# The end of a depthwise convolution on one core: who sums the last chunks' taps, and what the layer norm's queue holds

## The chip, the core and the metric

The kernel runs on one core of a Trainium2 chip. The metric is the device time of one execution in microseconds (us); the number for a kernel is the median of its runs. TensorE is called PE in the profile, VectorE DVE, ScalarE ACT, GpSimd POOL, and SyncE's queue, which issues the weight loads, SPq.

## The reference

A two-layer trunk over 256 tokens of width 2048, in float32. Layer 0 mixes with a convolution module, layer 1 with latent attention, and each is followed by a squared-ReLU MLP of width 8192. Only the convolution module of layer 0 matters here:

```python
def conv_module(h, w_pw1, b_pw1, w_dw, b_dw, ln_g, ln_b, w_pw2, b_pw2):
    u = h @ w_pw1 + b_pw1                     # 2048 -> 4096
    a, gate = jnp.split(u, 2, axis=-1)
    u = a * jax.nn.sigmoid(gate)
    u = causal_depthwise_conv(u, w_dw) + b_dw # 31 taps, every channel by itself
    u = jax.nn.silu(layer_norm(u, ln_g, ln_b))
    return u @ w_pw2 + b_pw2                  # 2048 -> 2048
```

The layer norm takes mean and variance over all 2048 channels of a token, so nothing of it, and nothing of the second product (pw2), can start before the last channel of the depthwise sum is there.

## The kernel before

**Numbers.** Products are done in split float32: each operand is cut into a high part (`hi`, a rounded copy made on ScalarE) and a low part (`lo` = value minus `hi`, made on VectorE or GpSimd), and three matmuls hi·hi, lo·hi and hi·lo are summed. `split_half` (L152) does this for one half of a loaded weight group: `hi` at L158, `lo` at L159. A loaded group lies in one of three `raw` buffers, and the next load into that buffer waits until both halves have been cut.

**Tiling.** Channels are cut into 16 chunks (`KC`) of 128, tokens into two tiles of 128. Until the layer norm, data lie with channels on partitions and the 256 tokens along the free axis (`S` = 256).

**The conv stage** (L703 to L733) loops over chunks `c`, with the order of the instructions on every engine written out by hand (`manual_schedule`). In turn `c`, PE computes the pw1 product of chunk `c` (`conv_mm`, L483), while the other engines work on the chunk before: `glu(c-1)` (L501) makes the gated value `ub` from two accumulators (the sigmoid on ACT; the product on GpSimd, but on VectorE for the last chunk, L509), and the 31 taps of the depthwise sum follow. Of an ordinary chunk:

- ScalarE does tap 0 with the bias (L542) and a few more taps as separate products (`product`, L519), which GpSimd adds up (`side_sum`, L562);
- VectorE does the other taps, one multiply-add of 128x256 each (`dve_tap`, L586), and adds the GpSimd sum once (L569). `dve_taps` (L590) takes turns between the two oldest chunks that have taps left, so that one multiply-add needn't wait for the one just before it. It stops when `REST` or `LAST_REST` taps are left over all chunks; what is left is done in the next turn.

The last chunk (number 15) is different. `LAST_PE` = 22 of its taps are matmuls with diagonal weights (`diag`, L524, made on ScalarE; `last_products`, L534), 11 ahead of the transposes of chunk 13 and 11 behind; four are ScalarE products added by GpSimd; five are on VectorE, which adds all three parts at L583.

**Queues at the end.** Turn 16 has no pw1 product. VectorE's queue holds `glu(15)`, then the rest of chunks 13, 14 and 15. PE's queue holds the matmul taps, the transposes of chunk 13 (`to_tokens`, L617; its statistics `bn_stats`, L633, follow on VectorE), the rest of the matmul taps, then some dummy transposes (`keep_warm`, L220, with the counts `N_WARM_LN`) and the transposes of chunks 14 and 15.

**The layer norm** (L738 to L791). `bn_aggr` (L743) gives mean and variance of each token; `rsqrt` (L201) the scale, by a square root on ScalarE and one Newton step on VectorE; `spread` (L748) puts mean and scale across partitions with PE transposes; `ln_op` subtracts the mean or multiplies by the scale (L763); `ln_swish` does the SiLU on ScalarE (L771), its high part `sh` (L774), and its low part `sl` on VectorE (L775). `rsqrt` is used by every RMS norm but the final one as well; one of those calls stands ahead of the first product of the kernel.

**The pw2 product** (L792) then runs over the 16 values of `k`, two to a weight group. `NU` = 32 is the number of the first pw2 weight group; the groups 32 and 33 are loaded and partly cut before the layer norm. In the kernel before, the second half of group 33 is cut inside the loop, behind `ln_swish(4)` in ScalarE's queue.

Of the kernel before, what the change touches and what calls it, by code (L numbers as in the profile page):

```python
# [43 lines left out]
LAST_PE = 22  # L44
SIDE = 2
LAST_SIDE = (3, 6, 4)
# [3 lines left out]
LAST_REST = (20, 17, 0)  # L50
FILL_AT = (5, 15)
N_WARM = 14
N_WARM_LN = (8, 17, 6, 10)
# [23 lines left out]
def trunk_kernel(  # L77
# [74 lines left out]
    def split_half(raw, h, eng):  # L152
# [5 lines left out]
        nc.scalar.activation(hi, raw[:, js, :], AF.Copy)  # L158
        eng.tensor_tensor(lo, raw[:, js, :], hi.bitcast(F32), op=ALU.subtract)  # L159
        return hi, lo  # L160

# [39 lines left out]
    def rsqrt(ms, n, eps, name):  # L201
# [8 lines left out]
        nc.vector.tensor_tensor(t, t, v, op=ALU.mult)  # L210
        nc.vector.tensor_scalar(t, t, scalar1=-0.5, scalar2=1.5, op0=ALU.mult, op1=ALU.add)
        nc.vector.tensor_tensor(y, y, t, op=ALU.mult)
# [224 lines left out]
    with ExitStack() as cx:  # L437
# [32 lines left out]
        def conv_half(n, h):  # L470
            if n < NU + KC // 2:
                wjs[n, h] = split_half(raws[n], h, nc.gpsimd if 0 < n + h and (n, h) < (NU + 1, 1) else nc.vector)
# [44 lines left out]
        def product(c, w):  # L517
            pr = cv2.tile([P, S], F32, tag="tp", name=nm("tp"), bufs=sum(LAST_SIDE))
            nc.scalar.activation(pr, ubs[c][:, w : w + S], AF.Copy, scale=tap(c, w))  # L519
            return pr  # L520
# [10 lines left out]

        def last_products(w0, w1):
            for w in range(w0, w1):
                nc.tensor.matmul(  # L534
                    last_sum[0], dgs[w], ubs[KC - 1][:, w : w + S], start=w == 0, stop=w == LAST_PE - 1
                )

        def start_sum(c):
            w = 0
            if c < KC - 1:  # L540
                pcs[c] = sum_tile()[:, :S]
                nc.scalar.activation(  # L542
                    pcs[c], ubs[c][:, 0:S], AF.Identity, bias=b_dw[:, c : c + 1], scale=tap(c, 0)
                )
                w = 1
            else:
                pcs[c] = acc_tile()[:, :S]
                o = sum_tile()[:, :S]
                last_sum.append(o)
                last_products(0, LAST_PE // 2)  # L550
                w = LAST_PE
            n = n_side(c)
            sides[c] = [product(c, w + i) for i in range(n)]
            left[c] = list(range(w + n, W))
            left[c].insert(min(JOIN, len(left[c]) - 1), None)
# [8 lines left out]

        def dve_tap(c):
            w = left[c].pop(0)
            out = pcs[c]
            if w is None:
                nc.vector.tensor_tensor(out, out, sides[c][0], op=ALU.add)  # L569
                return  # L570
            if c == KC - 1 and w == LAST_PE + n_side(c):
                nc.vector.tensor_scalar(
                    out, ubs[c][:, w : w + S], scalar1=tap(c, w), scalar2=b_dw[:, c : c + 1],
                    op0=ALU.mult, op1=ALU.add,
                )
                return
            if not left[c]:
                if c == KC - 1:
                    half = cv2.tile([P, S], F32, tag="half", name=nm("half"), bufs=1)
                    nc.vector.scalar_tensor_tensor(  # L580
                        out=half, in0=ubs[c][:, w : w + S], scalar=tap(c, w), in1=out, op0=ALU.mult, op1=ALU.add
                    )
                    nc.vector.tensor_tensor(ca[:, c, :], last_sum[0], half, op=ALU.add)  # L583
                    return
                out = ca[:, c, :]
            nc.vector.scalar_tensor_tensor(  # L586
                out=out, in0=ubs[c][:, w : w + S], scalar=tap(c, w), in1=pcs[c], op0=ALU.mult, op1=ALU.add
            )

        def dve_taps(c, fill):  # L590
# [3 lines left out]
            lead = 0 if c in (0, KC - 1) else LEAD  # L594
            while sum(len(v) for v in left.values()) > rest(c):
# [3 lines left out]
                if ready[-1] == KC - 1 and len(left[KC - 1]) == 1 and len(ready) > 1:  # L599

                    ready.pop()
                k = next((k for k in ready[:2] if k != last), None)
                if fill and (k is None or n >= FILL_AT[c == KC - 1]):
# [4 lines left out]
                if c == KC - 1 and k == KC - 3 and not left[k]:  # L608

                    to_tokens(k)  # L610
                    last_products(LAST_PE // 2, LAST_PE)
                last = turns["last"] = k
                n += 1
            while fill:
                fill.pop(0)()

# [30 lines left out]
        with tc.manual_schedule():  # L647
# [55 lines left out]
            for c in range(1, KC + 1):  # L703
# [4 lines left out]
                if c < KC:  # L708
                    pss[c] = [acc_tile() for _ in range(2)]
                conv_half(n + (c < KC), 0)  # L710
                start_sum(c - 1)
                if c < KC:
                    conv_half(n + 1, 1)
                    dve_taps(c - 1, fill)
                    conv_load(n + 4)
                    side_sum(c - 1)
                    conv_mm(c, 0, 8)
                    if c < KC - 1:
                        conv_half(n + 2, 0)
                        conv_half(n + 2, 1)  # L720
                else:
                    side_sum(c - 1)
                    conv_half(n, 1)
                    conv_half(n + 1, 0)
                    dve_taps(c - 1, fill)
                    conv_load(n + 4)
                if c < KC:
                    conv_mm(c, 8)
                    if c > KC - 4:
                        dgs.extend(diag(KC - 1, w) for w in range(len(dgs), min(len(dgs) + 8, LAST_PE)))  # L730
                    if c > 2:
                        to_tokens(c - 3)
                    conv_mm(c, 12)  # L733
# [19 lines left out]
            rl = rsqrt(mv[:, :, 1], T, LN_EPS, "n")  # L753
# [6 lines left out]
            def ln_op(k, n, row, op):  # L760
                o = ca[:, k : k + n, :]
                row = row.rearrange("p (a n) -> p a n", a=1).broadcast_to([P, n, S])
                nc.vector.tensor_tensor(o, o, row, op=op)  # L763

# [18 lines left out]
            for row, op in ((mean, ALU.subtract), (scale, ALU.mult)):  # L783
                for k in range(2):
                    ln_op(k, 1, row, op)
            for k in range(2):
                ln_swish(k, 1)
            ln_norm(2)
            ln_swish(2)
            ln_norm(4)  # L790
            keep_warm(ident, N_WARM_LN[3])  # L791
            for m in range(NP):  # L792
# [4 lines left out]
                for j in range(2):  # L797
                    k = 2 * m + j
                    wh, wl = conv_w(NU + m, j)
                    for b in range(2):  # L800
                        bs = slice(b * NB, (b + 1) * NB)
                        for t in range(T):
                            mm3(ps2[b][t], sh_kt(k, t), sl_kt(k, t), wh[:, bs], wl[:, bs], k == 0, k == KC - 1)
                    if m == 0 and j == 0:
                        conv_half(NU + 1, 1)
# [600 lines left out]
```

## Time and profile before

| | us |
|---|---|
| median of three runs (lowest, highest) | 1997.01 (1995.37, 1997.14) |
| the profiled execution: its own time | 1997.01 |
| the profiled execution: span from the first to the last instruction | 1995.1 |
| PE busy, share of the span | 1970.5, 99% |
| DVE busy | 1219.0, 61% |
| ACT busy | 972.5, 49% |
| POOL busy | 223.9, 11% |
| mean granted TensorE clock | 0.998 |

Times in the views count from the start of the span. A row of the timeline gives start, duration, engine, line, operation, output and inputs, shapes, the count of instructions merged into the row, and in brackets how long the engine had been idle and what ended that. A float32 matmul of the depthwise taps (L534) stands in the trace as two records, so 22 records are 11 taps. The conv stage ends near 204 us, its depthwise sum near 218, and the pw2 product starts near 223.5.

### The profile page before, as it was taken

The numbers are of one execution on the slowest core, as the hardware profiler recorded it, in microseconds if no ns is written. First come the engines' busy times: TensorE is split into PE (matmuls) and PEld (weight loads), VectorE is DVE, ScalarE is ACT, GpSimd is POOL, SyncE is SP. The second block draws the span as 40 slices with busy tenths as digits, with TensorE's granted clock in tenths as the row PEclk, the third lists the DMA queues.
The fourth block names the chain that finished last, engine by engine and source line by source line (L and its number), as shares of the span: only waits on it lengthen the run. The fifth ranks groups of instructions, "written<-read, shape, count | busy, mean of one in ns | idle before, by whom it ended". The sixth has DMA issues, their size and how long they took to land.

```text
span 1995.1 us, 27788 instructions
## 1 busy us (share of the span) xinstructions
PE 1970.5 (99%) x11025; PEld 1726.1 (87%) x11025; DVE 1219.0 (61%) x1808; ACT 972.5 (49%) x1378; POOL 223.9 (11%) x184
## 2 busy tenths in 40 slices
PE   7999999999999999999999999999999999999998
PEld 7999788888888888888899998888888888888886
DVE  6999877556444555655556665656654545665553
ACT  5456655445333444544456665545443334454443
POOL 5999200000000000000001310000000000000000
PEclk9999999999999999999999999999999999999999
DMA  7666365665655666655555445666655666655553
GB/s 239 186 182 183 127 208 179 189 190 189 198 198 191 190 190 190 190 190 190 190 159 174 122 148 183 198 190 190 191 190 191 197 194 189 190 190 196 194 190 105
DMA packets 243265, 367.57 MB, mean 184 GB/s; under 512 B 15416, under 2 KB 89792, under 8 KB 242880
## 3 DMA queue, kind: packets, MB, share of 16 engines
q1 hardware_dynamic: 242400, 364.68, 58.0%
q8 instruction: 86, 1.41, 0.3%
q10 hardware_dynamic: 736, 1.12, 0.2%
q14 instruction: 43, 0.35, 0.0%
HBM read 363.68 MB, written 2.10 MB: 183 GB/s over the span
## 4 chain that ended last, share of the span: by engine, by line
PE 89%; DVE 8%; ACT 1%; DMA 0%; issue 0%; POOL 0%; SPq 0%; ACTq 0%; DVEq 0%
PE acc L403 23%; PE acc L184 16%; PE acc L186 16%; PE acc L185 16%; PE acc L404 12%; DVE sum L586 6%; PE acc L490 1%; PE acc L489 1%; PE acc L491 1%; PE tr L241 1%; PE sum L534 1%; DMA xs<-in_x 0%; ACT hi L158 0%; DVE lo L159 0%; PE acc L1180 0%
## 5 line engine op out<-in xcount | busy, mean ns | idle before, releaser
L159 DVE TENSOR_TENSOR lo<-raw,hi 128x1024 fp32r<-128x1024 f32 (+2 forms) x630 | 760.9, 1211 | 691.3 <-ACT hi L158 679.5
L158 ACT ACTIVATE hi<-raw 128x1024 fp32r<-128x1024 f32 (+1 forms) x696 | 723.3, 1046 | 790.0 <-PE acc L185 454.8
L403 PE MATMUL acc<-xt,hi 128*128 128x512 f32 x2048 | 710.6, 390 | 0.0
L404 PE MATMUL acc<-xt,lo 128*128 128x256 f32 x2048 | 577.7, 282 | 0.0
L403 PEld LDWEIGHTS acc<-xt,hi 128*128 128x128 f32 x2048 | 384.5, 188 | 80.5
L184 PE MATMUL acc<-hi,gh 128*128 128x512 f32 x1024 | 398.6, 389 | 0.0
L186 PE MATMUL acc<-lo,gh 128*128 128x512 f32 x1024 | 398.4, 389 | 0.0
L185 PE MATMUL acc<-hi,gl 128*128 128x512 f32 x1024 | 398.4, 389 | 0.0
L404 PEld LDWEIGHTS acc<-xt,lo 128*128 128x128 f32 x2048 | 387.1, 189 | 0.1
L186 PEld LDWEIGHTS acc<-lo,gh 128*128 128x128 f32 x1024 | 192.2, 188 | 40.1
L184 PEld LDWEIGHTS acc<-hi,gh 128*128 128x128 f32 x1024 | 192.2, 188 | 40.0
L185 PEld LDWEIGHTS acc<-hi,gl 128*128 128x128 f32 x1024 | 192.2, 188 | 39.2
L586 DVE SCALAR_TENSOR_TENSOR sum<-ub,w_dw,sum 128x256 f32<-128x256 f32 x400 | 162.7, 478 | 7.5 <-ACT sum L542 6.4
L159 POOL TENSOR_TENSOR lo<-raw,hi 128x1024 fp32r<-128x1024 f32 x66 | 157.6, 2408 | 22.0 <-ACT hi L158 22.0
L489 PE MATMUL acc<-xt,hi 128*128 128x256 f32 x512 | 144.4, 282 | 0.0
L491 PE MATMUL acc<-xt,lo 128*128 128x256 f32 x512 | 143.0, 279 | 0.3 <-POOL lo L159 0.3
L490 PE MATMUL acc<-xt,hi 128*128 128x256 f32 x512 | 143.0, 279 | 0.2 <-DVE xt L197 0.2
L491 PEld LDWEIGHTS acc<-xt,lo 128*128 128x128 f32 x512 | 96.2, 188 | 0.5 <-POOL lo L159 0.5
L490 PEld LDWEIGHTS acc<-xt,hi 128*128 128x128 f32 x512 | 96.3, 188 | 0.4 <-DVE xt L197 0.4
L489 PEld LDWEIGHTS acc<-xt,hi 128*128 128x128 f32 x512 | 96.3, 188 | 0.0
L975 POOL MEMSET pad_kv<- 128x8 f32 x1 | 0.1, 105 | 769.2 <-PE acc L186 769.2
L411 ACT ACTIVATE v<-acc 128x256 f32<-128x256 f32 x128 | 46.3, 381 | 25.4 <-PE acc L404 25.4
(240 smaller groups left out, 1780.4 us busy)
## 6 DMA issues: line engine op xcount, KB each, us to landing
raw<-in_mlp_w SPq DMA_DIRECT2D x256, 1024.0 KB, 5.2
raw<-in_conv_w_pw SPq DMA_DIRECT2D x64, 512.0 KB, 5.3
raw<-in_conv_w_pw SPq DMA_DIRECT2D x16, 1024.0 KB, 5.1
raw<-in_mla_w_o SPq DMA_DIRECT2D x16, 1024.0 KB, 5.7
raw<-in_mla_w_kv_up SPq DMA_DIRECT2D x8, 1024.0 KB, 5.6
raw<-in_mla_w_in SPq DMA_DIRECT2D x8, 576.0 KB, 3.7
raw<-in_mla_w_in SPq DMA_DIRECT2D x4, 1024.0 KB, 5.5
raw<-in_mla_w_q_up SPq DMA_DIRECT2D x16, 256.0 KB, 3.5
```

Source lines behind the costliest of these rows:

```text
L158: nc.scalar.activation(hi, raw[:, js, :], AF.Copy)
L159: eng.tensor_tensor(lo, raw[:, js, :], hi.bitcast(F32), op=ALU.subtract)
L184: nc.tensor.matmul(ps, sh, mh, start=start, stop=False)
L185: nc.tensor.matmul(ps, sl, mh, start=False, stop=False)
L186: nc.tensor.matmul(ps, sh, ml, start=False, stop=stop)
L403: nc.tensor.matmul(ps[b], wh[:, bs], xhl(k), start=k == 0, stop=False)
L404: nc.tensor.matmul(ps[b][:, :S], wl[:, bs], xh(k), start=False, stop=k == KC - 1)
L411: nc.scalar.activation(v[:, b, :], o[:, S:], AF.Copy)
L489: nc.tensor.matmul(o, wh[:, bs], xh(k), start=k == 0, stop=False)
L490: nc.tensor.matmul(o, wh[:, bs], xl(k), start=False, stop=False)
L491: nc.tensor.matmul(o, wl[:, bs], xh(k), start=False, stop=k == KC - 1)
L586: nc.vector.scalar_tensor_tensor(out=out, in0=ubs[c][:, w : w + S], scalar=tap(c, w), in1=pcs[c], op0=ALU.mult, op1=ALU.add)
```

## The change

- **Last chunk's taps.** `LAST_PE` falls from 22 to 20: 20 taps on PE, in two halves of 10. The other 11 (20 to 30) are all ScalarE products, the first with the bias, and GpSimd adds them up with ten additions. VectorE only adds the PE part and the GpSimd part.
- **Gap.** Before its first matmul tap PE gets 12 dummy transposes (`N_WARM_GAP`).
- **Chunks 13 and 14.** `dve_taps(14)` leaves 20 items instead of 17, so `glu(15)` stands three multiply-adds earlier on VectorE. A new function `dve_end` does the rest: the last four taps of chunk 13 in turns with three of chunk 14, then the last twelve of chunk 14 as two separate sums in turns (one of them starting from chunk 14's GpSimd sum, so that L569 falls away), which one addition joins. The statistics of chunk 13 come after 14 multiply-adds.
- **Weight groups 32 and 33.** The first half of 32 is cut in turn 15 (ScalarE behind the halves of group 31, GpSimd ahead of chunk 14's `side_sum`); its second half in turn 16 behind chunk 15's products and additions. The high parts of both halves of 33 (`upper_half`) are made in turn 16 on ScalarE, their low parts (`lower_half`) on VectorE behind `ln_swish(2)`; before, the low part of the first half was on GpSimd.
- **Layer norm.** `rsqrt` has one VectorE instruction less; the first subtraction of the mean stands inside it, between the square root and the reciprocal; `ln_norm(4)` moves ahead of `ln_swish(2)`; the counts of dummy transposes change from (8, 17, 6, 10) to (6, 13, 7, 13).
- **Order of the terms.** In pw2, for `k` = 0 the matmuls with the low part of the activations (`sl`) come behind the others of that `k`, for `k` = 2 those with the low part of the weights.

```diff
-LAST_PE = 22
+LAST_PE = 20
-LAST_SIDE = (3, 6, 4)
+LAST_SIDE = (3, 6, W - LAST_PE)
-LAST_REST = (20, 17, 0)
-FILL_AT = (5, 15)
+LAST_REST = (20, 20)
+FILL_AT = (5, 14)
-N_WARM_LN = (8, 17, 6, 10)
+N_WARM_GAP = 12
+N_WARM_LN = (6, 13, 7, 13)
...
-    def rsqrt(ms, n, eps, name):
+    def rsqrt(ms, n, eps, name, meanwhile=None):
...
         nc.scalar.activation(t, v, AF.Sqrt)
+        if meanwhile is not None:
+            meanwhile()
         nc.vector.reciprocal(y, t)
-        nc.vector.tensor_tensor(t, y, y, op=ALU.mult)
+        nc.vector.scalar_tensor_tensor(out=t, in0=y, scalar=-0.5, in1=y, op0=ALU.mult, op1=ALU.mult)
         nc.vector.tensor_tensor(t, t, v, op=ALU.mult)
-        nc.vector.tensor_scalar(t, t, scalar1=-0.5, scalar2=1.5, op0=ALU.mult, op1=ALU.add)
-        nc.vector.tensor_tensor(y, y, t, op=ALU.mult)
+        nc.vector.scalar_tensor_tensor(out=y, in0=t, scalar=1.5, in1=y, op0=ALU.add, op1=ALU.mult)
...
+        def start_last():
+            c = KC - 1
+            last_sum.append(sum_tile()[:, :S])
+            keep_warm(ident, N_WARM_GAP)
+            last_products(0, LAST_PE // 2)
+            sides[c] = [product(c, w, None if w > LAST_PE else b_dw[:, c : c + 1]) for w in range(LAST_PE, W)]
...
+        def dve_end(fill):
+            c, d = KC - 3, KC - 2
+            n = 0
+            left[d].remove(None)
+            while left[c]:
+                dve_tap(c)
+                if left[c]:
+                    dve_tap(d)
+                    n += 1
+                n += 1
+
+            to_tokens(c)
+            last_products(LAST_PE // 2, LAST_PE)
+            m = len(left[d]) // 2
+            first, second = left[d][:m], left[d][m:]
+            left[d] = []
+            out = acc_tile()[:, :S]
+            half = cv2.tile([P, S], F32, tag="half", name=nm("half"), bufs=1)
+            for i, w in enumerate(second):
+                add_tap(half if i == len(second) - 1 else out, d, w, sides[d][0] if i == 0 else out)
+                if i < len(first):
+                    add_tap(pcs[d], d, first[i], pcs[d])
+                n += 2
+                while fill and n >= FILL_AT[1]:
+                    fill.pop(0)()
+            nc.vector.tensor_tensor(ca[:, d, :], pcs[d], half, op=ALU.add)
+            nc.vector.tensor_tensor(ca[:, d + 1, :], last_sum[0], sides[d + 1][0], op=ALU.add)
...
+                if c == KC:
+                    start_last()
+                    side_sum(KC - 1)
+                    conv_half(NU, 1)
+                    uppers = [upper_half(raws[NU + 1], h) for h in range(2)]
+                    dve_end(fill)
+                    conv_load(n + 4)
+                    break
...
+                if c == KC - 1:
+                    conv_half(NU, 0)
...
-            for row, op in ((mean, ALU.subtract), (scale, ALU.mult)):
-                for k in range(2):
-                    ln_op(k, 1, row, op)
+            ln_op(0, 1, scale, ALU.mult)
+            ln_norm(1, 1)
             for k in range(2):
                 ln_swish(k, 1)
             ln_norm(2)
+            ln_norm(4)
             ln_swish(2)
-            ln_norm(4)
+            for h in range(2):
+                wjs[NU + 1, h] = lower_half(*uppers[h], nc.vector)
             keep_warm(ident, N_WARM_LN[3])
...
+                    late = {0: 1, 2: 2}.get(k)
+                    groups = [terms] if late is None else [terms[:late] + terms[late + 1 :], [terms[late]]]
...
-                    if m == 0 and j == 0:
-                        conv_half(NU + 1, 1)
```

More of the change, by code (lines that the diff above doesn't have):

```diff
@@ L150, in load, with upper_half @@
         return raw
-    def split_half(raw, h, eng):
+    def upper_half(raw, h):
         _, nj, cols = raw.shape
@@ L563, in side_sum, with add_tap @@
                 step *= 2
+        def add_tap(out, c, w, base):
+            nc.vector.scalar_tensor_tensor(
+                out=out, in0=ubs[c][:, w : w + S], scalar=tap(c, w), in1=base, op0=ALU.mult, op1=ALU.add
+            )
         def dve_tap(c):
             w = left[c].pop(0)
-            out = pcs[c]
             if w is None:
[L569 to L588, printed above, removed]
+                nc.vector.tensor_tensor(pcs[c], pcs[c], sides[c][0], op=ALU.add)
+            else:
+                add_tap(pcs[c] if left[c] else ca[:, c, :], c, w, pcs[c])
         def dve_taps(c, fill):
             n, last = 0, turns.get("last")
-            lead = 0 if c in (0, KC - 1) else LEAD
+            lead = 0 if c == 0 else LEAD
             while sum(len(v) for v in left.values()) > rest(c):
```

111 lines of the change are left out of this document (50 added, 61 removed).

## Prediction, made before the changed kernel was run

> **What bounds the kernel now.** I began with the engines' shares on the page and with PE's waits from the start of pw2 to the end.
>
> ```profile
> PE 1970.5 (99%) x11025; PEld 1726.1 (87%) x11025; DVE 1219.0 (61%) x1808; ACT 972.5 (49%) x1378; POOL 223.9 (11%) x184
> ...
> PE tr L1171 <- DVE pr L1165: 1.2, 2, 1.0
> PE acc L184 <- ACT hi L158: 0.6, 1, 0.6
> PE acc L184 <- ACT sh L774: 0.6, 1, 0.6
> PE acc L186 <- DVE lo L159: 0.5, 1, 0.5
> ```
>
> PE is busy 99% of the span, and from 223 us on it waits five times, for 2.9 us together; the three waits of L184 and L186 (1.7 us) lie at the start of pw2, as rows below show. So whatever brings pw2 forward brings the end forward, and the place to look is between the last pw1 matmul and the steady part of pw2. There the share misleads: PE counts as busy, but at half clock or with dummy transposes. The chain that ended last, cut to that stretch, tells the order:
>
> ```profile
> 197.00 8.24 DVE sum L586 x21
> 205.24 0.41 DVE ub L509
> ...
> 205.69 6.70 PE sum L534 x22
> 212.39 0.22 PE tr L624 x2
> 212.61 4.75 PE sum L534 x22
> 217.36 0.87 PE acc L224 x8
> 218.24 0.45 PE acc L624 x4
> ...
> 218.71 0.76 DVE stats L633 x2
> ```
>
> VectorE works through chunks 13 and 14 until it can start `glu(15)`; then 22 matmul taps on PE hold everything until 217.36. The first 11 take 6.70 us, the same count behind them 4.75. The windows (PE, PEld, DVE, ACT, POOL busy, then the granted clock) say why:
>
> ```profile
> 206.00:207.00 1.00, 1.00 (x4) 0.86 (x3) 1.00 (x4) 1.00 (x4) 1.00 (x1) 0.61 0.06 16
> 208.00:209.00 1.00, 1.00 (x4) 0.82 (x3) 1.00 (x4) 1.00 (x2) 1.00 (x2) 0.50 0.00 0
> 210.00:211.00 1.00, 1.00 (x7) 0.86 (x6) 1.00 (x4) 0.77 (x2) 1.00 (x1) 1.00 0.00 0
> ```
>
> The clock is 0.61, 0.50 and then 1.00. What precedes is in the timeline:
>
> ```profile
> 203.38 0.28 PE L491 MATMUL acc<-xt,lo 128*128 128x256 f32 x1
> 203.76 0.47 ACT L506 ACTIVATE sg<-acc,vecs 128x256 f32<-128x256 f32 x1 [3.71 <-PE acc L491]
> 205.19 0.45 DVE L509 SCALAR_TENSOR_TENSOR ub<-acc,vecs,sg 128x256 f32<-128x256 f32 x1
> 194.84 2.50 ACT L519 ACTIVATE tp<-ub,w_dw 128x256 f32<-128x256 f32 x6
> 198.37 2.40 POOL L159 TENSOR_TENSOR lo<-raw,hi 128x1024 fp32r<-128x1024 f32 x1 [1.70 <-ACT hi L158]
> 200.73 3.63 POOL L562 TENSOR_TENSOR tp<-tp,tp 128x256 f32<-128x256 f32 x5
> 213.72 2.57 DVE L586 SCALAR_TENSOR_TENSOR sum<-ub,w_dw,sum 128x256 f32<-128x256 f32 x5
> ```
>
> PE's last pw1 matmul ends at 203.66 and its first tap starts at 205.69: 2.03 us of idle, and a stretch at half clock behind it. The sigmoid is there at 204.23, but VectorE takes it up at 205.19.
>
> **The change part by part.** All of this is against the profiled execution, 1995.1 us of span in 1997.01 us, which is also the median of the three runs (1995.37 to 1997.14).
>
> *The glu comes earlier.* A multiply-add in turns costs 8.24/21 = 0.392 us. Three fewer ahead of the glu free VectorE at 205.19 - 1.18 = 204.01, but the sigmoid ends at 204.23, so the glu starts at about 204.25: 0.94 earlier, not 1.18. PE's first tap stood 0.50 behind the glu's start, so `ub` allows it at 204.75.
>
> *The gap.* Twelve dummy transposes at 0.87/8 = 0.109 us fill 203.5 to 204.8. They are queued ahead of the taps and end about 0.1 us after `ub` is there: first tap at 204.87. With the clock held, ten taps cost 10 x 4.75/11 = 4.32 us; were it to drop all the same, 10 x 6.70/11 = 6.09. I take 4.32, since the drop follows the one idle stretch and the clock stays full in the later stretch that ends with dummy transposes. [...] The windows above show the drop behind a 2.03 us gap, so I go by them; the other case is a rival below.
>
> *The taps on PE.* 4.32 + 0.22 (transposes of chunk 13) + 4.32 = 8.86 us; PE is done at 204.87 + 8.86 = 213.73, where it was 217.36.
>
> *The taps on ScalarE and GpSimd.* ScalarE's products cost 2.50/6 = 0.42; eleven from 204.75 on end at 209.3, and the additions use them two by two, so they aren't late. GpSimd gets the low half of group 32 ahead of chunk 14's five additions: it is free of group 31 at 200.77, does this one (2.40) until 203.15 and the five additions (3.63) until 206.8. Then come the ten additions at 3.63/5 = 0.726: 206.8 + 7.26 = 214.05. This row carries the price well: same shape, same neighbours. So GpSimd, not PE, ends last, by 0.3 us.
>
> *VectorE.* From 204.61 (0.36 behind the glu's start) seven multiply-adds reach 207.36, where the second sum of chunk 14 needs the GpSimd sum of 206.8: 0.6 us to spare, and if GpSimd were later the whole rest of VectorE's queue would wait behind that instruction. Twelve more and two statistics of about 0.34 give 212.7; the joining addition ends near 213.25. One sum alone would have paid 2.57/5 = 0.51 for each tap, which is why there are two. VectorE is under the cover of GpSimd by about 0.8 us.
>
> So L583 starts at about 214.1 (GpSimd) instead of behind 217.36. Six dummy transposes end at 214.3, ahead of that; in the kernel before eight ended at 218.23 and held the transposes back. Now the last two transposes run at 214.57 and the statistics start at about 214.98, where they started at 218.71: **3.73 us**.
>
> *The layer norm.*
>
> ```profile
> 219.39 0.58 DVE L743 BATCH_NORM_AGGREGATE mv<-stats 128x2 f32<-128x48 f32 x2
> 220.84 0.17 DVE t L210
> 221.04 0.18 DVE t L211
> 221.32 1.41 DVE L763 TENSOR_TENSOR ca<-ca,tr 128x256 f32<-128x256 f32 x4
> 223.53 0.50 PE L184 MATMUL acc<-hi,sh 128*128 128x512 f32 x1 [0.55 <-ACT sh L774]
> 223.99 0.50 PE L185 MATMUL acc<-hi,sl__119 128*128 128x512 f32 x1
> ```
>
> A Newton instruction costs 0.20 (220.84 to 221.04); one goes. But the subtraction that moved in front of the reciprocal waits for the mean to be spread, which takes about 0.4 us from the end of `bn_aggr` (an estimate from the 0.22 of two transposes and the waits around them), and the instruction itself takes 1.41/4 = 0.35; until now that time was covered by the square root alone. I reckon the reciprocal 0.33 later, the scale 0.13 later, and so pw2: **-0.13** (ends: -0.35 and +0.2). The thirteen transposes (1.42 us) end at about the time the mean is there.
>
> *The first low part.* For `k` = 0 PE's second matmul stood 0.46 behind its first, waiting for `sl`; another comes first now and follows in about 0.3: **0.15**.
>
> *The stall of group 33.*
>
> ```profile
> 231.84 0.39 PE L186 MATMUL acc<-lo,sh 128*128 128x512 f32 x1
> 232.83 0.50 PE L184 MATMUL acc<-hi,sh 128*128 128x512 f32 x1 [0.60 <-ACT hi L158]
> 234.42 0.40 PE L184 MATMUL acc<-hi,sh 128*128 128x512 f32 x1
> 224.80 1.40 DVE L763 TENSOR_TENSOR ca<-ca,tr 128x512 f32<-128x512 f32 x2
> 228.03 0.69 DVE L775 TENSOR_TENSOR sl__119<-ca,sh 128x512 fp32r<-128x512 f32 x1 [1.83 <-ACT sh L774]
> 231.73 2.94 ACT L158 ACTIVATE hi<-raw 128x1024 fp32r<-128x1024 f32 x3
> 232.81 3.50 DVE L159 TENSOR_TENSOR lo<-raw,hi 128x1024 fp32r<-128x1024 f32 x3 [0.25 <-ACT hi L158]
> ```
>
> At the pace of 0.227 us (231.84 to 232.07) the fourth matmul of `k` = 3 would stand at 232.07 + 3 x 0.227 = 232.75; it stands at 234.42, because the high part of group 33's second half is cut behind `ln_swish(4)` and the low part behind that. Now both high parts (0.98 each) are made before the layer norm, on a ScalarE that is done with them near 212.2; the table load for the square root behind them ends near 213.7, and the root is needed past 216. What is late next? VectorE, which does `ln_norm(2)`, `ln_norm(4)` (1.40 each, 1.33 in a row), `sl` (0.69) and two low parts (1.17 each) in that order. With pw2 at 219.93, `sl(2)` is ready at 225.1 and needed at 225.7; the low parts of 33 at 226.3 and 227.5, needed at 227.3 and 228.7; the first of 34 at 230.7, needed at 231.4. Everything is in time by 0.6 to 1.2 us, so the stall goes: **1.67**. If the cover fails it comes back, at most in full.
>
> On SP's queue the load of group 35 waits for the second half of 32, which GpSimd now cuts behind the ten additions (near 216.5); PE needs that group past 236, and a later load (36) is released earlier, since the low part of 33 is done at 227.5 and not past 234. No loss.
>
> *The other calls of `rsqrt`.* Ahead of the first matmul one instruction less: **0.20**; the rest are off the path, by PE's waits above.
>
> Sum: 3.73 - 0.13 + 0.15 + 1.67 + 0.20 = 5.62 us. 1997.01 - 5.6 = **1991.4 us**.
>
> **The rivals.**
>
> *The clock isn't held by dummy transposes.* PE ends 1.77 later, at 215.5, and so ahead of GpSimd no more: 1.4 later than my 214.1. Gain 4.2, **1992.8**. This is the case in which the drop has another cause than the idle stretch and the ten taps cost 6.09. Against it: the clock of 0.61 directly behind that stretch. [...]
>
> *The stall of pw2 only moves.* `ln_norm(4)` and the low parts now stand ahead of `sl(4)` and group 34 on VectorE; margins of 0.6 us are small beside queues of 6 us. If the 1.67 comes back: gain 3.95, **1993.1**.
>
> *GpSimd becomes the bound: slower.* Fifteen additions in a row stand between 203.15 and the last chunk. The time is no better than before from the point where they cost the 5.6 us: 0.726 + 5.6/15 = 1.10 us each. At twice their price (1.45) the end moves by 10.9 us to **2002.3**. The nearest other GpSimd row bounds it: 2.40 for four times the elements. For it: VectorE runs beside them all the time. Against it: it did beside the five additions at 200.73 too. [...]
>
> *The change does nothing it says.* The glu could be held by the sigmoid later than 204.23, and the layer norm lose its 0.35; both together leave a gain of 4 to 5, so no case by itself.
>
> **How the numbers follow.** 0.2%, 4.0 us, is about what a measurement of this kernel can tell from no change. My forecast, with its ends (PE the bound instead of GpSimd, layer norm at its better end: gain 6.3; worse ends: 4.7), gets 0.68; the clock rival 0.09; the moved stall 0.14; GpSimd as bound 0.05; some wait that I don't see and that eats most of the gain 0.04. Faster than 1993.0: the forecast, the clock rival and a part of the moved stall, 0.80. Within 0.2%: the rest of the moved stall and the unseen wait, 0.15. Slower: 0.05. The range goes from 6.3 of gain, and 0.9 below that for the scatter of the runs (1.77 between lowest and highest), to the moved stall and 0.5 of scatter: 1989.8 to 1993.6.
>
> **What would show it.** Right: the first matmul tap near 204.9; ten taps in 4.3 us with the clock at 1.00 from 203 to 214; the last GpSimd addition near 214; statistics near 215; pw2 near 220; no wait of PE on group 33; then the same distance to the end as before. Wrong: a clock under 1.00 past 205, a wait of VectorE on `side_sum` of chunk 14, a wait of L583 on GpSimd by several us, or a new wait of PE on `sl` or `lo` in the first four `k`.

## The result and the profile after

| | us |
|---|---|
| before, median of 11 runs (lowest, highest) | 1997.00 (1995.12, 1997.14) |
| after, median of 11 runs (lowest, highest) | 1991.26 (1991.09, 1991.42) |
| ratio after/before, 95% interval | 0.9975 [0.9966, 0.9983] |
| the profiled execution of after: its own time, span | 1991.36, 1989.4 |

The forecast was 1991.4. The times of the kernel before fall in two groups with nothing between them, 1995.12 to 1995.52 (4 of 11) and 1996.88 to 1997.14 (7 of 11), and the execution profiled before was one of the upper group; the changed kernel has one group. The experiments come back to that.

The chain that ended last, of the changed kernel (start, duration, what):

```profile
203.48 1.31 PE acc L233 x12
204.79 4.42 PE sum L547 x20
209.22 0.22 PE tr L643 x2
209.44 4.32 PE sum L547 x20
213.76 0.65 PE acc L233 x6
214.41 0.44 PE acc L643 x4
...
216.57 0.42 DVE ca L776
...
219.27 0.42 ACT sh L793
219.73 30.44 PE acc L829 x133
```

PE's first tap stands at 204.79, its last ends at 213.76, and pw2 begins at 219.73, where it began at 223.53. VectorE no longer stands in this chain ahead of the taps. The windows (PE, PEld, DVE, ACT, POOL busy, then the granted clock) have the full clock where it was 0.61 and 0.50:

```profile
205.00:207.00 2.00, 2.00 (x11) 1.76 (x10) 2.00 (x6) 2.00 (x6) 1.92 (x4) 1.00 0.05 14
207.00:209.00 2.00, 2.00 (x11) 1.74 (x10) 2.00 (x5) 2.00 (x6) 2.00 (x4) 1.00 0.00 0
```

The timeline, VectorE and then GpSimd:

```profile
204.09 0.48 DVE L518 SCALAR_TENSOR_TENSOR ub<-acc,vecs,sg 128x256 f32<-128x256 f32 x1
207.23 0.95 DVE L577 SCALAR_TENSOR_TENSOR acc<-ub,w_dw,tp 128x256 f32<-128x256 f32 x1
208.09 0.48 DVE L577 SCALAR_TENSOR_TENSOR sum<-ub,w_dw,sum 128x256 f32<-128x256 f32 x1
213.86 0.42 DVE L634 TENSOR_TENSOR ca<-sum,tp 128x256 f32<-128x256 f32 x1 [0.26 <-PE sum L547]
214.88 0.76 DVE L652 BATCH_NORM_STATS2 stats<-acc 128x6 f32<-128x256 f32 x2 [0.60 <-PE acc L643]
216.18 0.17 DVE L214 TENSOR_SCALAR v<-mv 128x2 f32<-128x2 f32 x1
202.90 10.78 POOL L573 TENSOR_TENSOR tp<-tp,tp 128x256 f32<-128x256 f32 x15
213.64 2.37 POOL L163 TENSOR_TENSOR lo<-raw,hi 128x1024 fp32r<-128x1024 f32 x1
```

The statistics start at 214.88 (before: 218.71). The last addition of the taps waited 0.26 us for PE. GpSimd's fifteen additions end at 213.68, VectorE's own sums at 213.60, PE's taps at 213.76: the three engines finish within 0.16 us. PE's waits from 195 us to the end have no row for group 33 any more (left out is L1198, two waits of 1.2 us together, which the kernel before has too, there L1171):

```profile
PE tr L769 <- DVE y L221: 0.4, 1, 0.4
PE acc L500 <- POOL lo L163: 0.3, 1, 0.3
PE acc L829 <- ACT sh L793: 0.2, 1, 0.2
```

Where the time came from, as starts before minus starts after: the end of the pw1 matmuls 0.18 (203.66 to 203.48), the statistics 3.83, the start of pw2 3.80, the fourth matmul of `k` = 3 5.71 (234.42 to 228.71), the span 5.7. All of it is there by `k` = 3.

The runs of the experiments below were made on three chips, each beside the kernel before, whose two groups lay within 0.2 us of the same places on all three. So a difference of 0.2 us or less against the 1991.26 of the changed kernel (called after below) means nothing.

### The profile page after: what moved, and what is told of

Its sections match the earlier page's. It is cut to its first block, busy times and chain, and to the rows that moved or that the text cites. A ratio compares the mean times of both kernels' runs of the same rounds, so it can differ in the third digit from the quotient of the medians.

```text
span 1989.4 us, 27794 instructions
## 1 busy us (share of the span) xinstructions
PE 1967.4 (99%) x11031; PEld 1724.8 (87%) x11031; DVE 1217.0 (61%) x1796; ACT 975.0 (49%) x1383; POOL 226.5 (11%) x190
## 4 chain that ended last, share of the span: by engine, by line
PE 90%; DVE 6%; ACT 1%; POOL 1%; issue 0%; DMA 0%; SPq 0%; ACTq 0%; POOLq 0%; DVEq 0%
PE acc L412 23%; PE acc L194 15%; PE acc L192 15%; PE acc L193 15%; PE acc L413 12%; DVE sum L577 5%; PE acc L829 2%; PE acc L500 1%; PE acc L499 1%; PE acc L498 1%; PE tr L250 1%; POOL lo L163 1%; PE sum L547 0%; ACT hi L159 0%; DMA xs<-in_x 0%
## 5 line engine op out<-in xcount | busy, mean ns | idle before, releaser
L163 DVE TENSOR_TENSOR lo<-raw,hi 128x1024 fp32r<-128x1024 f32 (+1 forms) x631 | 762.0, 1211 | 691.0 <-ACT hi L159 679.3
```

The source lines that it names most:

```text
L163: eng.tensor_tensor(lo, raw, hi.bitcast(F32), op=ALU.subtract)
```

## The experiments

**after_again.** The changed kernel once more, beside 31 runs of the kernel before.

> The changed kernel once more, as the base on this chip for the runs beside it. Both theories: 1991.3 us, as its first runs gave; the span 1989.4.

Measured 1991.25 (1991.11 to 1991.39); before 1995.24 to 1995.53 in 16 runs and 1996.86 to 1997.18 in 15; ratio 0.9976 [0.9967, 0.9985]. The two groups of before came again, and the one of after. So the median of before means little; against its lower group the change gains 4.1 us, against the upper one 5.8.

**before_again and before_third.** The kernel before, unchanged, each with a profile.

> The kernel before once more, for its profile. Its times fall into two groups, near 1995.3 and near 1997.0, while the changed kernel and the kernel before with the idle stretch filled have one. Theory (the 2.03 us idle stretch costs the clock in some executions and not in others): a time near 1995.3 shows a granted clock of 1.00 behind the stretch and 4.8 to 5.0 us for the first 11 taps; a time near 1997.0 shows 0.5 to 0.6 and 6.7 us. Rival (the groups come from elsewhere): the clock drops in both.

> The same kernel before, one more execution, for the same question: near 1995.3 with the clock at 1.00, or near 1997.0 with a drop; the rival expects the drop in both.

1995.31 and 1995.34, both of the lower group. The windows and the timeline of before_again:

```profile
206.00:207.00 1.00, 1.00 (x6) 0.87 (x6) 1.00 (x4) 1.00 (x4) 1.00 (x1) 1.00 0.00 0
208.00:209.00 1.00, 1.00 (x6) 0.88 (x5) 1.00 (x4) 1.00 (x2) 1.00 (x2) 1.00 0.00 0
```

```profile
205.75 5.02 PE L534 MATMUL sum<-ub,dg 128*128 128x256 f32 x22 [2.06 <-DVE ub L509]
210.83 4.92 PE L534 MATMUL sum<-ub,dg 128*128 128x256 f32 x22
```

2.06 us of idle, as in the execution profiled before (2.03), and the clock stays at 1.00: the first 11 taps take 5.02 us and not 6.70. before_third shows the same (2.07 us of idle, the clock at 1.00, 5.02 us). So the two groups differ by this stretch at half clock, 1.7 us. Three executions were profiled, one with the drop and two without; of all others only the time tells the group. By their times, an idle stretch of that length cost the clock in about half of the executions (15 of the 31 above).

**gap_only.** Of the whole change only a fill of the gap, in the kernel before.

```diff
                 last_sum.append(o)
+                keep_warm(ident, 18)
```

> The kernel before with one edit: 18 dummy transposes (18 x 0.109 = 1.96 us) between the last pw1 matmul and the first matmul tap, in the 2.03 us in which PE was idle. Theory (the idle stretch costs the clock): granted clock 1.00 from 204 to 212, the first 11 taps take 4.75 instead of 6.70 us, chunk 13's transposes come 1.95 earlier and VectorE's wait of 1.20 us for them goes, so VectorE ends 1.2 us earlier and PE 1.95; VectorE is then the later of the two, the last sum starts near 216.1 instead of 217.4, and the time falls by about 1.3 us only (1995.7). [...]

1995.37 (1995.17 to 1995.58), ratio 0.9997 [0.9987, 1.0006]: one group, at before's lower one. The windows and the timeline:

```profile
207.00:208.00 1.00, 1.00 (x7) 0.86 (x6) 1.00 (x4) 1.00 (x2) 1.00 (x2) 1.00 0.00 0
```

```profile
205.68 5.02 PE L534 MATMUL sum<-ub,dg 128*128 128x256 f32 x22
210.75 4.92 PE L534 MATMUL sum<-ub,dg 128*128 128x256 f32 x22
215.42 0.48 DVE L581 SCALAR_TENSOR_TENSOR half<-ub,w_dw,acc 128x256 f32<-128x256 f32 x1
```

With the gap filled the clock stayed, by their times, in all ten runs, which is worth 1.7 us in those executions that would have lost it, and nothing in the others. VectorE's last multiply-add ends at 215.90 and PE's taps at 215.67 (210.75 + 4.92): with the clock held, the kernel before is bound by both nearly alike, and a fill alone has nothing more to give.

**no_gap.** The changed kernel without the fill.

```diff
-            keep_warm(ident, N_WARM_GAP)
```

> The changed kernel without the 12 dummy transposes ahead of the matmul taps. PE is then idle from about 203.5 to 204.6, for 1.1 us instead of the 2.03 of the kernel before. Theory 1 (any idle stretch of about that size costs the clock): clock 0.5 to 0.6 from 205 to 209, ten taps 6.1 instead of 4.4 us, PE ends near 215.4 instead of 213.8, time +1.6 us (1992.9). Theory 2 (it takes a longer stretch, somewhere between 1.1 and 2.0 us here): clock 1.00, taps 4.3 us, PE ends 0.1 us earlier than with the fill, time the same within 0.2 us.

1991.29 (1991.13 to 1991.42), ratio 0.9975 [0.9966, 0.9985]. No difference, and one group. The windows and the timeline:

```profile
204.00:205.00 1.00, 0.32 (x1) 0.30 (x2) 0.90 (x4) 0.45 (x2) 1.00 (x3) 1.00 0.88 356
206.00:207.00 1.00, 1.00 (x7) 0.86 (x6) 1.00 (x4) 1.00 (x4) 1.00 (x2) 1.00 0.00 0
```

```profile
204.68 4.58 PE L547 MATMUL sum<-ub,dg 128*128 128x256 f32 x20 [1.14 <-DVE ub L518]
```

PE idles for 1.14 us, and by their times none of the ten runs lost the clock. The fill in the changed kernel is worth nothing: the earlier glu, which shortens the gap, does it alone.

**old33.** Group 33 cut as before (low part of the first half on GpSimd, second half in the loop), all else changed.

```diff
-                    uppers = [upper_half(raws[NU + 1], h) for h in range(2)]
+                    conv_half(NU + 1, 0)
...
-            for h in range(2):
-                wjs[NU + 1, h] = lower_half(*uppers[h], nc.vector)
...
+                if m == 0:
+                    conv_half(NU + 1, 1)
```

> The changed kernel with weight group 33 cut as in the kernel before: first half in turn 16 (low part on GpSimd), second half inside the pw2 loop behind ln_swish(4) on ScalarE. Theory (that place in the queues was the stall): PE waits for the high part and then the low part of group 33 at k = 3, near 228 to 230, and the time rises by up to 1.67 us (1992.9). Rival (ln_norm(4) ahead of ln_swish(2) alone lets ScalarE reach ln_swish(4) early enough): the high part is cut near 226, ahead of its need at 228.0, and the time stays at 1991.3.

1993.17 (1992.98 to 1994.38), ratio 0.9988 [0.9979, 0.9998]: 1.9 slower than after, about the size that the stall would have, but by another way. PE had no wait on group 33. The timeline, VectorE and GpSimd:

```profile
215.59 0.58 DVE L762 BATCH_NORM_AGGREGATE mv<-stats 128x2 f32<-128x48 f32 x2
216.21 2.13 DVE L214 TENSOR_SCALAR v<-mv 128x2 f32<-128x2 f32 x1
213.65 4.67 POOL L163 TENSOR_TENSOR lo<-raw,hi 128x1024 fp32r<-128x1024 f32 x2
```

`v`, an instruction on two elements a partition, takes 2.13 us where it took 0.17, and ends at 218.34, with GpSimd's second 128x1024 instruction (213.65 + 4.67 = 218.32), which had started at 215.96, ahead of it. `bn_aggr` ahead of it ran beside GpSimd undisturbed (0.58 us, as in the kernel before, where GpSimd was idle then). PE then waits 2.1 us for `y`. Four of the ten runs were 1.1 us longer still (in balance below, where PE waits 2.3 us at this place, three were 1.2 to 1.4 longer); a clock lost in this wait of PE, as behind the 2.03 us of idle in the kernel before, would fit, but none of those was profiled.

**lock_free.** To tell these apart: old33, but the low part of group 33's first half on VectorE, so that GpSimd is free when `v` comes; the second half still in the loop.

```diff
-                    uppers = [upper_half(raws[NU + 1], h) for h in range(2)]
+                    uppers = [upper_half(raws[NU + 1], 0)]
...
+                if m == 0:
+                    conv_half(NU + 1, 1)
```

> Weight group 33 cut half as in the kernel before, half as changed: the high part of its second half is made inside the pw2 loop behind ln_swish(4), as before; the low part of its first half is made on VectorE behind ln_swish(2), as changed, so that GpSimd's last work is the second half of group 32. With the first low part on GpSimd as well (the run old33) the time was 1.9 us longer, not by a wait of PE on group 33 but by one VectorE instruction of two elements (v, 2.13 us) that ended together with GpSimd's last instruction. Theory (that instruction and GpSimd shut each other out, and the early high parts are not what removed the stall): v takes 0.17 us again, PE waits for nothing in pw2, time 1991.3. Rival (the late cut of the second half costs the 1.9 us in some way): 1993.1.

1992.12 (1991.99 to 1992.47), ratio 0.998 [0.9971, 0.9989]. The timeline, VectorE and PE:

```profile
216.17 0.17 DVE L214 TENSOR_SCALAR v<-mv 128x2 f32<-128x2 f32 x1
228.24 0.39 PE L828 MATMUL acc<-hi,sl__119 128*128 128x512 f32 x1
229.15 0.50 PE L828 MATMUL acc<-lo,sh 128*128 128x512 f32 x1 [0.52 <-DVE lo L163]
```

`v` is back at 0.17, as the theory said, but the time came between the two forecasts. What is left is 0.87; PE's wait on the second low part of group 33 makes up 0.68 of it (229.15, where 228.24 and a step of 0.227 give 228.47), and slower steps behind the wait another 0.15 (27 steps take 6.27 us, in after 6.12). So with `v` undisturbed the early cut is worth 0.87. The two costs don't add up: in old33 pw2 began 1.71 late (221.44 instead of 219.73), which gave the late cut the time that it needed, so that PE didn't wait for group 33. Clearing GpSimd out of the way of `v` took 1.05 off old33, less than the 1.71, because the late cut then showed.

**taps18.** 18 taps on PE, 13 on ScalarE and GpSimd.

```diff
-LAST_PE = 20
+LAST_PE = 18
```

> The changed kernel with 18 taps of the last chunk on PE and 13 on ScalarE and GpSimd (instead of 20 and 11). PE's taps end 2 x 0.432 = 0.86 us earlier, near 212.9; GpSimd has two additions more, 2 x 0.72 = 1.44 us, and ends near 215.1 instead of 213.7. Theory (PE at 213.8 and GpSimd at 213.7 are level in the changed kernel, so that either one moved later moves the end): the last sum waits for GpSimd until 215.1, time +1.3 us (1992.6). Rival (GpSimd has slack, PE alone is the bound): the last sum starts when PE or VectorE is done, time -0.2 to -0.8 us.

1992.39 (1992.23 to 1992.69), 1.1 slower than after. The timeline, GpSimd and VectorE:

```profile
203.15 12.14 POOL L573 TENSOR_TENSOR tp<-tp,tp 128x256 f32<-128x256 f32 x17
215.32 0.42 DVE L634 TENSOR_TENSOR ca<-sum,tp 128x256 f32<-128x256 f32 x1 [1.48 <-POOL tp L573]
```

Two additions more at 0.714 each make GpSimd the bound, and VectorE waits 1.48 us for it. So GpSimd stands right at the edge of being the bound, as the theory here had it. The price of each addition stayed; the prediction's rival had needed a higher one.

**balance.** 19 taps on PE; the low part of 32's first half behind the additions on GpSimd, and the additions in the order in which ScalarE's products arrive.

```diff
-LAST_PE = 20
+LAST_PE = 19
...
-                    side_sum(KC - 1)
+                    for i, j in ((0, 1), (2, 3), (0, 2), (4, 5), (6, 7), (4, 6), (0, 4), (8, 9), (10, 11), (8, 10), (0, 8)):
+                        nc.gpsimd.tensor_tensor(ps[i], ps[i], ps[j], op=ALU.add)
+                    wjs[NU, 0] = lower_half(*upper32, nc.gpsimd)
```

> A try at a better version: 19 taps on PE and 12 on ScalarE and GpSimd; GpSimd cuts the low part of the first half of group 32 behind the additions instead of ahead of chunk 14's, and takes chunk 15's products in the order in which they come. PE ends 0.43 us earlier (213.3), GpSimd starts 2.4 us earlier with one addition more and ends near 213.4, VectorE stays at about 213.5 and becomes the bound. Theory: time -0.3 us (1991.0). Rival (chunk 14's and 15's additions now run at other times beside VectorE, or group 32 comes late for pw2): no gain or a loss of up to 1 us.

1993.59 (1993.38 to 1994.93), 2.3 slower, where I had hoped for a little less than after. The timeline, GpSimd and VectorE:

```profile
205.62 8.58 POOL L731 TENSOR_TENSOR tp<-tp,tp 128x256 f32<-128x256 f32 x11 [1.54 <-ACT tp L529]
214.16 4.66 POOL L163 TENSOR_TENSOR lo<-raw,hi 128x1024 fp32r<-128x1024 f32 x2
216.49 2.36 DVE L214 TENSOR_SCALAR v<-mv 128x2 f32<-128x2 f32 x1
```

The additions wait for ScalarE's products and end no earlier, and the second 128x1024 instruction now stands beside `v`, which takes 2.36 us and ends with it (218.85 and 218.82). As in old33, `v` is shut out until GpSimd is done, from another edit.

**sbuf_acc.** The second sum of chunk 14 in SBUF instead of PSUM, so that each of its multiply-adds has two SBUF inputs.

```diff
-            out = acc_tile()[:, :S]
+            out = cv2.tile([P, S], F32, tag="part", name=nm("part"), bufs=1)
```

> The changed kernel with the second sum of chunk 14 kept in SBUF instead of PSUM, so that all six of its multiply-adds on VectorE read two inputs from SBUF while GpSimd adds; in the changed kernel only the first does, and the next instruction started 0.86 us behind it instead of 0.39. [...] Rival A (the 0.86 was a single late release by GpSimd of the sum it reads, not contention): multiply-adds stay at 0.39, time the same. [...]

1991.93 (1991.83 to 1992.09), 0.7 slower. I had expected 2.0: five more such instructions at the 0.47 us that the one in after loses (0.86 less 0.39), 2.3 us together, would have kept VectorE busy until about 216, past PE's 213.76. The timeline, VectorE and GpSimd (the last two rows are single additions out of the fifteen):

```profile
207.30 0.91 DVE L577 SCALAR_TENSOR_TENSOR part<-ub,w_dw,tp 128x256 f32<-128x256 f32 x1
208.13 0.47 DVE L577 SCALAR_TENSOR_TENSOR sum<-ub,w_dw,sum 128x256 f32<-128x256 f32 x1
208.53 0.56 DVE L577 SCALAR_TENSOR_TENSOR part<-ub,w_dw,part 128x256 f32<-128x256 f32 x1
209.00 0.48 DVE L577 SCALAR_TENSOR_TENSOR sum<-ub,w_dw,sum 128x256 f32<-128x256 f32 x1
202.95 11.70 POOL L573 TENSOR_TENSOR tp<-tp,tp 128x256 f32<-128x256 f32 x15
207.20 0.72 POOL L573 TENSOR_TENSOR tp<-tp,tp 128x256 f32<-128x256 f32 x1
207.88 0.92 POOL L573 TENSOR_TENSOR tp<-tp,tp 128x256 f32<-128x256 f32 x1
```

The first multiply-add with two SBUF inputs starts inside the addition that ends at 207.92 and ends at 208.21; the second starts inside the addition that ends at 208.80 and ends at 209.09. All six of them end 0.28 to 0.29 us behind the addition that was running when they started, and the addition that follows takes 0.90 to 0.92 us instead of 0.73. So the two engines do hold each other up, and what it costs VectorE depends on how much of the addition is left: the first is followed 0.83 us later by the next instruction, the others 0.47 to 0.49 later, because from then on they start when the addition is nearly done. A multiply-add with one SBUF input between them stays at 0.39 to 0.40. I had taken the 0.47 us that the first one loses for the price of each, and so the forecast came out too high. What lengthened the kernel was GpSimd: its additions cost 0.78 on the average and not 0.72 and end at 214.65 instead of 213.68, and VectorE's last sum waits 0.57 us for them.

The same reading explains the 0.86 in after: there the instruction starts at 207.23, inside an addition that ends at 207.89, and ends 0.29 behind it, at 208.18. In balance the same instruction, with the same inputs, starts between two additions (the one ahead of it ends at 207.14) and takes 0.49; the next follows 0.40 behind its start. VectorE and GpSimd in balance:

```profile
207.16 0.49 DVE L577 SCALAR_TENSOR_TENSOR acc<-ub,w_dw,tp 128x256 f32<-128x256 f32 x1
206.41 0.73 POOL L731 TENSOR_TENSOR tp<-tp,tp 128x256 f32<-128x256 f32 x1
```

**ln_old.** The layer norm's edits and the order of the terms undone, all else changed.

```diff
-N_WARM_LN = (6, 13, 7, 13)
+N_WARM_LN = (8, 17, 6, 10)
...
-            rl = rsqrt(mv[:, :, 1], T, LN_EPS, "n", lambda: ln_op(0, 1, mean, ALU.subtract))
+            rl = rsqrt(mv[:, :, 1], T, LN_EPS, "n")
...
-                    late = {0: 1, 2: 2}.get(k)
+                    late = None
```

(and the Newton step with four VectorE instructions, in every `rsqrt`)

> The changed kernel with the layer norm's own edits undone: rsqrt with its old instructions and nothing inside it, both subtractions of the mean ahead of both multiplications, the old order of the matmul terms for k = 0 and 2, the old counts of dummy transposes (8, 17, 6, 10). The cutting of weight groups stays as changed. Theory, by steps: one rsqrt instruction more ahead of the first matmul 0.20; two more dummy transposes ahead of chunk 14's transposes 0.22; from the statistics to pw2 4.82 instead of 4.85, -0.03; the wait for sl at k = 0 0.12. Sum +0.5 us (1991.8). Rival (these edits are worth as much as the taps): +1.5 us or more.

1992.18 (1992.02 to 1992.30), 0.9 slower, where 0.5 had been expected. The timeline of PE:

```profile
220.12 0.49 PE L831 MATMUL acc<-hi,sh 128*128 128x512 f32 x1 [0.55 <-ACT sh L794]
220.57 0.50 PE L831 MATMUL acc<-hi,sl__119 128*128 128x512 f32 x1
...
226.19 0.39 PE L831 MATMUL acc<-hi,sl__119 128*128 128x512 f32 x1
226.49 0.50 PE L831 MATMUL acc<-lo,sh 128*128 128x512 f32 x1
226.83 0.40 PE L831 MATMUL acc<-hi,sh 128*128 128x512 f32 x1
```

Of the 0.9, 0.39 is there at pw2's start (0.19 from the root ahead of the first product, the rest from the longer row of dummy transposes, which holds chunk 14's and 15's back until 214.82), and 0.47 comes behind it: matmul 37 of pw2 stands 8.77 behind the first and not 8.30. 0.26 of that is there by `k` = 2, from the wait for `sl` at `k` = 0 (0.45 between the first two matmuls); the other 0.21 is a delay inside `k` = 2, where the low part of group 33 comes too late for the old order (226.49 and 226.83 instead of steps of 0.227). The expectation had no term for it. From the statistics to pw2 it took 4.83 us, after 4.85: the layer norm's own edits make no difference.

**root_direct.** An attempt at something faster than after: the square root straight from the variance, with the small constant as ScalarE's bias from a new tile of 128x1, the subtraction behind the Newton step.

```diff
+    ln_eps = const.tile([P, 1], F32, name="ln_eps")
...
+        nc.scalar.activation(t, ms, AF.Sqrt, bias=ln_eps)
+        nc.scalar.activation(v, ms, AF.Identity, bias=ln_eps)
```

> A try at a better version: the changed kernel, but the layer norm's square root takes the variance directly with LN_EPS as its bias, ScalarE also makes v, and the subtraction of the mean for chunk 0 stands behind the reciprocal square root. VectorE's v (0.20 us) leaves the chain and the reciprocal no longer waits for the mean to be spread (216.57 to 216.90 in the changed kernel): by steps the scale is ready 0.49 us earlier. Theory: time -0.5 us (1990.8). Rival (chunk 0's subtraction then comes too late for its multiplication, or PE's dummy transposes hold the spread): -0.2 us or nothing.

2002.87, and 2009.9 in two of five runs, one of them the profiled one; ratio 1.0041 [1.0026, 1.0055]. The stretch itself got shorter as expected: from the statistics to the first `sh` 4.07 us, in after 4.39. But a line far away got longer. The groups by line and form of root_direct, and then of after:

```profile
L428 PE MATMUL acc<-xt,hi 128*128 128x512 f32 x2048 | 724.1, 399 | 0.0
```

```profile
L412 PE MATMUL acc<-xt,hi 128*128 128x512 f32 x2048 | 710.5, 390 | 0.0
```

The same 2048 matmuls of an MLP take 13.6 us more, and the pw1 stage some 5 (`glu(15)` at 209.33, after 204.09). The new tile stands ahead of nearly all others of its pool and moves them. That the placement does it is argued, not shown, nor why two runs are 7 us longer; a version that keeps every tile in its place was not run.

## Why the prediction was right, and where it wasn't

**What held.** The sum: 5.62 forecast, 5.7 measured against the same profiled execution. The terms, forecast and measured (the 0.18 of the root taken off the 3.83 for the statistics; the first low part by the first matmul of `k` = 1, which stood 3.09 behind the start of pw2 and now 2.86; the stall from there to the fourth matmul of `k` = 3, 7.80 and now 6.12):

| term | forecast | measured |
|---|---|---|
| statistics earlier | 3.73 | 3.65 |
| layer norm | -0.13 | -0.03 |
| first low part | 0.15 | 0.23 |
| stall of group 33 | 1.67 | 1.68 |
| root ahead of the first product | 0.20 | 0.18 |

The glu's start (204.25 forecast, 204.09), the ten taps (4.32 each, 4.42 and 4.32), PE's end (213.73, 213.76) and the additions (0.726, 0.719) came as reckoned from rows of the same shape.

**The gap: right number, wrong reason.** I credited the dummy transposes with holding the clock. no_gap shows them to be worth nothing: the glu, 1.10 earlier (205.19 to 204.09), leaves 1.14 us of idle, which by their times cost the clock in none of ten runs. That the idle stretch was behind the drop was right all the same: gap_only, with the gap filled, kept the clock in ten of ten. But the step "the drop follows the one idle stretch" took one execution for all: in about half of them 2.03 us of idle cost nothing. So 1.7 of the 5.6 is a gain of a part of the executions; against the others the change gains 4.1. That the execution I worked from lay in the upper group, with the median of three runs, was chance. Against before_again, where the clock held, the statistics come 2.21 earlier (217.09 to 214.88). PE's chain has all of it: the first tap 0.96 earlier (205.75 to 204.79, the 0.18 of the root included), the taps with chunk 13's transposes 1.02 shorter (9.99 and 8.97, two taps fewer), and two dummy transposes fewer 0.22. No run changes the taps alone. Why one idle stretch costs the clock in one execution and not in the next stays open.

**GpSimd as the last by 0.3 us.** The last was PE, 0.08 behind GpSimd. GpSimd's first additions began 0.25 earlier than I put them, and each cost 0.007 less. VectorE was not 0.8 ahead of it but level: the first tap of the second sum cost 0.86 instead of 0.39. It is the one that reads two SBUF inputs, and the forecast had no price of its own for that. It ended 0.29 us behind the GpSimd addition that was running when it started (208.18 and 207.89), as all six such instructions did in sbuf_acc (0.28 to 0.29). The forecast of the statistics held because the engine that was last ended within 0.3 us of my 214.05, at 213.76. That it was another engine than I had said did no harm, which is luck.

**Group 33: the size right, the parts not.** I said that the early high parts take the stall away. lock_free puts the early cut of the second half at 0.87. The other 0.8 (1.67 less 0.87) I put down to `ln_norm(4)` ahead of `ln_swish(2)`, since with it neither lock_free nor old33 waits for a high part, for which the kernel before waited 0.6 us. This is argued: no run moves `ln_norm(4)` alone. And ln_old shows that 0.21 hang on the new order of terms at `k` = 2. My times at which the low parts were needed had that order in them, but I gave it no term of its own.

**What I did not see.** Taking the low part of 33 off GpSimd does more than feed pw2: with it there `v` is shut out until GpSimd is done (in old33 it took 2.13 us instead of 0.17 and ended 0.02 us behind GpSimd). In after GpSimd ends at 216.01 and `v` starts at 216.18. The margin is 0.17 us, and with one more 128x1024 instruction on GpSimd at that moment the kernel was 1.9 and 2.3 us slower, as old33 and balance show. None of my rivals had it. I had weighed GpSimd beside VectorE for the multiply-adds alone, and had put the end of GpSimd's cut near 216.5 without asking what VectorE does then. With `v` 1.30 behind the start of the statistics, as it came out, my 214.98 puts it at 216.28, inside that cut: by my own figures it would have been held up. That it wasn't, since GpSimd was done 0.5 earlier than I had reckoned, is luck.

**The layer norm.** The reciprocal stands 0.72 behind `v`, in ln_old 0.44: 0.28 later, where I had 0.33. The saved Newton instruction gives 0.20 back, so the scale lost about 0.08, and pw2 in the end 0.03 (4.85 from the statistics, before 4.82), where I had 0.13.

**The rivals.** A clock that isn't held would have stood in the windows; it didn't. The stall that only moves would have been a wait of PE on `lo` in the first four `k`; there is none in after, while lock_free has it. GpSimd as the bound came only with two additions more, in taps18, and cost 1.1 us there, far from that rival's 2002.3.

## What to carry to other kernels

When a stage ends on several engines, profile the kernel before more than once: a stretch at a low clock may be there in half of the executions (here, by their times, in 15 of 31), and a gain read from one of them is then half a gain. Before a filler is put into a gap, try to shorten the gap; here that did all (with 1.14 us of idle instead of 2.03, none of ten runs lost the clock by its time). Behind a GpSimd instruction of microseconds, look which VectorE instruction of the critical chain starts next, and keep GpSimd empty there, however small that instruction is: `v` on 128x2 elements took 2.13 and 2.36 us instead of 0.17. Where the two run side by side, look at the single GpSimd instructions and not at their merged row; the merged row hid who waited for whom.

## What the runs showed of the hardware

- An idle of PE of 2.03 us cost the clock in some executions of the same kernel, judged by their times (7 of the first 11, 15 of 31 beside after_again, 18 of 31 and 8 of 14 on the two other chips), and 1.14 us in none of ten. Granted clock behind it, in the three that were profiled: down to 0.50 in one, 1.00 in two.
- A VectorE instruction on 128x2 elements with one source took 2.13 and 2.36 us beside a 128x1024 GpSimd instruction that had started ahead of it (old33, balance), and ended with it within 0.03 us; in after, behind GpSimd's end, it took 0.17. What holds it back no run shows.
- All six VectorE multiply-adds with two SBUF inputs in sbuf_acc ended 0.28 to 0.29 us behind the GpSimd addition that was running when they started, and the addition that followed took 0.90 to 0.92 us instead of 0.73. The multiply-adds with one SBUF input between them stayed at 0.39 to 0.40 us.
- One small tile more in a pool went with 9 ns more for each of 2048 matmuls elsewhere (399 and 390 ns, one profiled execution of each kernel); the cause is open.
